# Strassen gate/up products: GpSimd sums spread out, weight conversions three products ahead, a fourth low-part buffer

## The chip, the core and the metric

The kernel runs on one core of one Trainium2 chip. The metric is the device time of one execution in microseconds (us); the median of three runs counts. The engines are written as in the profile: PE (TensorE matmul) with PEld (its weight loads), DVE (VectorE), ACT (ScalarE), POOL (GpSimd), SP (SyncE, which here issues DMAs).

## What is computed

One layer of a hybrid decoder on 512 prompt positions and 8 x 4 sample positions (544 columns in all): attention and a state-space branch, an output projection, then a SwiGLU feed-forward part, then a norm. All in float32. The change touches the last stages:

```python
hf = rms_norm(x, p['norm_ffn'][l])
x = x + (jax.nn.silu(hf @ p['w_gate'][l]) * (hf @ p['w_up'][l])) @ p['w_down'][l]
```

with a model width of 2048 and an inner width of 5632.

## The kernel before

**Precision.** A float32 operand is split in a high part (ACT copies it to float32r, "hi") and a low part (DVE subtracts, "lo"); a product is hi x hi + hi x lo + lo x hi, so three matmuls per 128x128 weight tile. `conv(u)` makes both parts of one weight block of 128x512: `wh` on ACT (L1994) and `wl` on DVE (L1995).

**Strassen.** A 256-row block of an output is made of seven products P1 to P7 (Winograd's form), each over weight blocks or sums of them. The sums of weight blocks are `sadd`: P5's and P6's on POOL (L1972, L1974), P7's and P3's on DVE (L1976, L1978). P6's sum reads P5's, P3's reads P6's. A product is a *unit*: 12 matmuls of 272 columns. Gate and up have two k halves, h0 and h1, so 14 units each, in the order `TWO`: P1.0 P5.0 P2.0 P1.1 P5.1 P6.0 P6.1 P3.0 P7.0 P7.1 P2.1 P4.0 P3.1 P4.1. In this text they are G0 to G13 for gate and U0 to U13 for up; G and U together are a *pair* of 28 units, and there are 22 pairs. Down has one half and seven units, D0 to D6 (P1 P5 P6 P2 P7 P3 P4), in 40 such groups: 32 with four k tiles (12 matmuls a unit), then 8 with three (9 matmuls a unit).

**PSUM.** P1, P6, P7 and P4 add into one bank X, P5 and P3 into Y, P2 into V. Since they add on, P7 may write X only after P6's running sum has been read out, and P4 only after P7's. The readers are *events*: in gate/up on ACT for P1, P5, P6, P7 (L2046, L2049, L2053, L2056), on DVE for P2, P3, P4; in down on ACT for P1, P5, P6 (L2178, L2182, L2187), on DVE for P2 (L2194), P7 (L2191), P3 (L2197), P4 (L2200).

**The order of the work** is written by hand. Every engine runs its instructions in the order in which `stage` emits them and waits for semaphores alone. For each unit u that is:

```python
for f in at.pop(u, ()):      # what plan_at put here
    f()
for v in sum_at.pop(u, ()):  # weight sums of later units
    sadd(v)
mms(u)
events(u - 1)
conv(u + 2)
```

`plan_at` puts the element-wise work of a pair (scaling by the norm's factor L2081, SiLU L2084, gate times up L2095, the four sums of the finished block L2107 to L2116, and the splits `one` and `two` of the forms that down will read, L387 on ACT and L388 on DVE) at chosen units; the DMA stores of those forms (`store`) too. For pairs 19 to 21 there are two plain splits (`direct`) in place of sums and splits. `AHEAD` says how many units early a sum is emitted.

**Buffers.** `wh` and `wl` rotate over three buffers each, the sums over four (tag `raw`; P6.1 has one of its own), the loaded weight halves `rw` over three. The next load is issued by `conv` of P4, which is the last reader.

Of the kernel before, what the change touches and what calls it, by code (L numbers as in the profile page):

```python
# [8 lines left out]
F32R = mybir.dt.float32r  # L9
# [3 lines left out]
ALU = mybir.AluOpType  # L13
# [4 lines left out]
P = 128  # L18
# [13 lines left out]
NK = 2  # L32
# [99 lines left out]
def hybrid_step(  # L132
# [9 lines left out]
    def nm(p):  # L142
        uid[0] += 1
        return f"{p}{uid[0]}"
# [4 lines left out]
    stream = es.enter_context(tc.tile_pool(name="stream", bufs=3))  # L149
# [7 lines left out]
    pools = {"act": actp, "ps": ps_p, "mm": mm_p}  # L157
# [1717 lines left out]
    PT = nc.gpsimd.tensor_tensor  # L1875
# [46 lines left out]
    units = []  # L1922
    raws = []

    AHEAD = {("P5", 0): 5, ("P6", 0): 8, ("P5", 1): 5, ("P6", 1): 6}
    at = {}
    sum_at = {}

    def add(g):
        gems.append(g)  # L1930
        g.u0 = len(units)
        for i, (p, h) in enumerate(g.order):
            last = all(q != p for q, _ in g.order[i + 1:])
            if p in ("P5", "P6", "P7", "P3"):
                e = AHEAD.get((p, h), 3) if len(g.halves) == 2 else 3
                sum_at.setdefault(max(len(units) - e, -1), []).append(len(units))
            units.append((g, p, h, i, last))
        for h in range(len(g.halves)):
            raws.append((g, h))
# [3 lines left out]
    def raw_dma():  # L1943
        if nraw[0] < len(raws):
            g, h = raws[nraw[0]]
            nraw[0] += 1
            k0, n, _ = g.halves[h]
            t = pools["wraw"].tile([P, 8, 256], F32, tag="wraw", name=nm("rw"))
            for a in range(0, 2 * n, 4):
                c = min(4, 2 * n - a)  # L1950
                nc.sync.dma_start(
                    out=t[:, a:a + c, :],
                    in_=g.W[(k0 + a) * P:(k0 + a + c) * P, g.c0:g.c0 + 256].rearrange("(k p) c -> p k c", p=P),
                )
            g.raw[h] = t

    def blk(g, h, i, j):
        n = g.halves[h][1]
        return g.raw[h].rearrange("p (j e) c -> p j e c", e=2)[:, 0:n, j, i * P:(i + 1) * P]

    def v128(t, n):
        return t.rearrange("p a (b c) -> p (a b) c", c=P)[:, 0:n]
# [22 lines left out]
    def conv(u):  # L1985
        if u >= len(units):
            return
        g, p, h, _, _ = units[u]
        n = g.halves[h][1]
        src = {"P1": lambda: blk(g, h, 0, 0), "P2": lambda: blk(g, h, 0, 1), "P4": lambda: blk(g, h, 1, 1)}.get(p, lambda: g.Sp.pop((p, h)))()  # L1990
        hi = stream.tile([P, NK, 256], F32R, tag="whi", name=nm("wh"))
        lo = stream.tile([P, NK, 256], F32R, tag="wlo", name=nm("wl"))
        hv, lv = v128(hi, n), v128(lo, n)
        nc.scalar.activation(out=hv, in_=src, func=AF.Copy)  # L1994
        TT(out=lv, in0=src, in1=hv.bitcast(F32), op=ALU.subtract)  # L1995
        conv_t[u] = hv, lv
        if p == "P4":
            raw_dma()

    def mms(u):  # L2000
        g, p, h, _, last = units[u]
        hv, lv = conv_t.pop(u)
        n = g.halves[h][1]
        new = BANK[p] not in g.b
        ps = g.bank(BANK[p])
        xs = [tuple(x.bitcast(F32R) for x in form(g.halves[h][2][j], FORMS[p])) for j in range(n)]
        todo = [(hv, j, x) for j in range(n) for x in xs[j]] + [(lv, j, xs[j][0]) for j in range(n)]
        for i, (w, j, x) in enumerate(todo):
            nc.tensor.matmul(ps[:, :HALF], lhsT=w[:, j, :], rhs=x, start=new and i == 0,  # L2009
                             stop=last and i == len(todo) - 1, skip_group_check=True)  # L2010
# [7 lines left out]
    def stage(u0, u1):  # L2018
        for u in range(u0, u1):
            for f in at.pop(u, ()):  # L2020
                f()
            for v in sum_at.pop(u, ()):
                sadd(v)
            mms(u)
            events(u - 1)
            conv(u + 2)
            g, _, _, i, _ = units[u]
            if i in g.hooks:
                g.hooks[i]()
            tick()  # L2030
# [37 lines left out]
    def gate_up(f):  # L2068
        gt, ut = [None] * 2, [None] * 2
        halves = [(0, 4, xforms[0:4]), (8, 4, xforms[4:8])]  # L2070

        def plan_at(u, *fs):
            for i, f_ in enumerate(fs):
                if f_ is not None:
                    at.setdefault(u + i, []).append(f_)

        def g4(g):
            TT(out=gt[1][:, L_], in0=g.b["X"][:, :HALF], in1=rbf[:, L_], op=ALU.mult)

        def scale(t):  # L2080
            return lambda: PT(out=gt[t], in0=gt[t], in1=rbf, op=ALU.mult)  # L2081

        def silu(t):
            return lambda: nc.scalar.activation(out=gt[t], in_=gt[t], func=AF.Silu)  # L2084

        def u4(g):
            TT(out=ut[1][:, L_], in0=g.b["X"][:, :HALF], in1=gt[1][:, L_], op=ALU.mult)

        def post_gate(u0):
            plan_at(u0 + 12, lambda: PT(out=gt[1][:, R_], in0=gt[1][:, R_], in1=rbf[:, R_], op=ALU.mult))  # L2090
            plan_at(u0 + 16, scale(0), silu(1), scale(1), silu(0), scale(0))

        def post_up(u0):
            plan_at(u0 + 12, lambda: PT(out=ut[1][:, R_], in0=ut[1][:, R_], in1=gt[1][:, R_], op=ALU.mult))
            plan_at(u0 + 16, lambda: PT(out=ut[0], in0=ut[0], in1=gt[0], op=ALU.mult))  # L2095
            pr = f // 2
            if pr < NPAIR:
                o = [None] * 7
                w = {}

                def store(*xs):
                    for x in xs:
                        nc.sync.dma_start(out=fd[pr, x], in_=o[x].bitcast(F32))

                def sum0():
                    w["t"], w["v"] = slot(), slot()
                    PT(out=w["t"][:, L_], in0=ut[0][:, R_], in1=ut[0][:, L_], op=ALU.subtract)  # L2107

                def sum1():
                    PT(out=w["v"][:, L_], in0=ut[1][:, R_], in1=ut[0][:, R_], op=ALU.subtract)  # L2110

                def sum2():
                    PT(out=w["t"][:, R_], in0=ut[1][:, R_], in1=w["t"][:, L_], op=ALU.subtract)

                def sum3():
                    PT(out=w["v"][:, R_], in0=ut[1][:, L_], in1=w["t"][:, R_], op=ALU.subtract)  # L2116

                def one():
                    o[0] = slot(F32R)
                    split((o[0][:, L_], o[0][:, R_]), ut[0][:, L_])  # L2120

                def two(x, src):
                    def go():
                        o[x], o[x + 1] = slot(F32R), slot(F32R)
                        split((o[x], o[x + 1]), src())
                    return go

                plan_at(u0 + 17, sum0, sum1, sum2, sum3)
                plan_at(u0 + 18, one, two(1, lambda: ut[1]), lambda: store(0, 1, 2), two(3, lambda: w["t"]),
                        two(5, lambda: w["v"]), lambda: store(3, 4, 5, 6))  # L2130
            else:
                def direct(x):
                    def go():
                        h, l = slot(F32R), slot(F32R)
                        split((h, l), ut[x])
                        for y, t in enumerate((h, l)):
                            nc.sync.dma_start(out=hd[f - (NF - NDIR) + x, y], in_=t.bitcast(F32))
                    return go
                plan_at(u0 + 17, direct(1), direct(0))

        ev = {}
        tmp_ev(ev, gt)
        ev["P4"] = g4
        add(Gem(W_G, f * P, halves, ev))
        post_gate(gems[-1].u0)
        ev = {}
        tmp_ev(ev, ut)
        ev["P4"] = u4
        add(Gem(W_U, f * P, halves, ev))
        post_up(gems[-1].u0)  # L2150

    for f in range(0, NF, 2):
# [106 lines left out]
    for c in range(nS):  # L2259
        for q in range(8):  # L2260
            g = units[nG + (c * 8 + q) * 7][0]
# [59 lines left out]
    for m in range(0, 16, 2):  # L2321
        if m == 10:
            flush()
            es_big2.close()
            pools["wraw"] = es_raw.enter_context(tc.tile_pool(name="wraw", bufs=3))
            for _ in range(3):
                raw_dma()

        def first_units(k):
            if k == 6:  # L2330
                for u in sum_at.pop(-1):
                    sadd(u)
                for u in range(2):
                    conv(u)

        run(gemm_pair(SXP, evac_ws(m), pre_piece=first_units if m == 14 else None))
# [161 lines left out]
```

## Time and profile before

| | us |
|---|---|
| median of three runs (lowest, highest) | 2196.16 (2195.12, 2199.06) |
| the profiled execution, its time | 2197.69 |
| its span on the core | 2195.8 |
| PE, PEld, DVE busy | 2065.0, 2007.4, 1848.8 |
| ACT, POOL busy | 1088.0, 1144.6 |

Gate/up runs from 696 to 1674 us, down from 1674 to 2088 us. Matmuls overlap each other, so a PE row of 12 matmuls is longer than the 1.5 us after which the next unit starts; starts are what to compare. A DVE row also runs some 0.08 us into the next one; again the distance of starts tells what the engine spends. POOL's ends are rough.

### The profile page before, as it was taken

To read this page: it belongs to the slowest core of one execution; us is meant where nothing else is said; L and a number is where in the kernel's file an instruction comes from. 1 tells how busy PE (TensorE), PEld (TensorE's weight loads), DVE (VectorE), ACT (ScalarE), POOL (GpSimd) and SP (SyncE) were. 2 spreads that over 40 slices of the span, in tenths; PEclk is the share of its full clock that TensorE was granted. 3 is DMA by queue.
4 is the path that set the end of the run, shared out by engine and by line. 5 is a ranking of instruction groups with operands and counts; after the bars stand their busy time and mean duration, and the time that the engine had idled before them with its cause. 6 is when DMAs were issued, how large, how long until landed. Compare 5 with 4: busy or idle time off the path is not lost.

```text
span 2195.8 us, 43890 instructions
## 1 busy us (share of the span) xinstructions
PE 2065.0 (94%) x16370; PEld 2007.4 (91%) x16370; DVE 1848.8 (84%) x2825; ACT 1088.0 (50%) x2277; POOL 1144.6 (52%) x1012
## 2 busy tenths in 40 slices
PE   8598899989998999999999999999999999999996
PEld 7587899879988899999999999999998999999995
DVE  7988845668577899999999999999997888888986
ACT  6143336764344455555555555555554445545564
POOL 7825433022275566656666666666655555555600
PEclk9798999999998999999999999999999999999998
DMA  6345794213342343434343434343439988977554
GB/s 187 110 131 159 230 274 126 62 59 116 116 155 90 111 154 113 152 133 166 113 151 134 166 114 151 131 162 120 151 118 320 324 287 282 345 268 237 190 162 140
DMA packets 331647, 368.46 MB, mean 168 GB/s; under 512 B 55473, under 2 KB 260249, under 8 KB 331417
## 3 DMA queue, kind: packets, MB, share of 16 engines
q1 hardware_dynamic: 330536, 363.92, 50.5%
q8 instruction: 128, 2.10, 0.4%
q0 software_dynamic: 640, 1.48, 0.2%
q14 instruction: 87, 0.70, 0.1%
q10 hardware_dynamic: 256, 0.26, 0.0%
HBM read 277.67 MB, written 88.52 MB: 167 GB/s over the span
## 4 chain that ended last, share of the span: by engine, by line
PE 62%; DVE 16%; issue 6%; ACT 2%; POOL 2%; DMA 1%; DVEq 0%; ACTq 0%; SPq 0%; POOLq 0%
PE mm L2009 44%; PE mm L293 15%; DVE wl L1995 8%; DVE sa L1976 2%; DVE s L388 1%; DVE sa L1978 1%; ACT wh L1994 1%; PE ps L1368 1%; POOL sa L1972 1%; DVE wl L263 1%; DMA rw<-in_w_up_dram 1%; PE ps L1626 0%; PE ps L1620 0%; DMA raw<-in_w_out_dram 0%; POOL s L2281 0%
## 5 line engine op out<-in xcount | busy, mean ns | idle before, releaser
L2009 PE MATMUL mm<-s,wh 128*128 128x272 f32 x7056 | 1040.0, 289 | 16.2 <-DVE s L2191 6.3
L2009 PEld LDWEIGHTS mm<-s,wh 128*128 128x128 f32 x7056 | 946.8, 189 | 23.2 <-ACT wh L1994 8.0
L2009 PE MATMUL mm<-s,wl 128*128 128x272 f32 x3528 | 597.3, 291 | 19.0 <-DVE wl L1995 17.1
L293 PE MATMUL mm<-s,wh 128*128 128x272 f32 x2816 | 508.2, 300 | 45.4 <-DVE u L1158 17.1
L2009 PEld LDWEIGHTS mm<-s,wl 128*128 128x128 f32 x3528 | 499.7, 189 | 33.2 <-DVE wl L1995 32.9
L1995 DVE TENSOR_TENSOR wl<-sa,wh 128x512 fp32r<-128x512 f32 (+1 forms) x468 | 482.0, 1040 | 53.5 <-ACT wh L1994 50.6
L293 PEld LDWEIGHTS mm<-s,wh 128*128 128x128 f32 x2816 | 418.3, 195 | 58.4 <-issue 31.7
L1995 DVE TENSOR_TENSOR wl<-rw,wh 128x512 fp32r<-128x512 f32 (+1 forms) x384 | 399.9, 1050 | 53.4 <-ACT wh L1994 52.9
L1994 ACT ACTIVATE wh<-sa 128x512 fp32r<-128x512 f32 (+1 forms) x468 | 291.5, 623 | 288.3 <-PE mm L2009 122.6
L293 PE MATMUL mm<-s,wl 128*128 128x272 f32 x1408 | 315.8, 295 | 25.3 <-DVE wl L263 25.1
L1994 ACT ACTIVATE wh<-rw 128x512 fp32r<-128x512 f32 (+1 forms) x384 | 236.7, 622 | 162.8 <-PE mm L2009 117.3
L1972 POOL TENSOR_TENSOR sa<-rw 128x512 f32<-128x512 f32 (+1 forms) x128 | 200.9, 1570 | 190.7 <-DVE wl L1995 116.1
L293 PEld LDWEIGHTS mm<-s,wl 128*128 128x128 f32 x1408 | 234.8, 195 | 27.5 <-DVE wl L263 27.5
L261 ACT ACTIVATE wh<-raw 128x512 fp32r<-128x512 f32 x200 | 124.4, 625 | 165.4 <-PE mm L293 98.1
L263 DVE TENSOR_TENSOR wl<-raw,wh 128x512 fp32r<-128x512 f32 x152 | 114.5, 758 | 82.9 <-ACT wh L261 82.7
L388 DVE TENSOR_TENSOR s<-s,s 128x544 fp32r<-128x544 f32 (+2 forms) x154 | 118.2, 784 | 40.8 <-ACT s L387 34.3
L1974 POOL TENSOR_TENSOR sa<-sa,rw 128x512 f32<-128x512 f32 (+1 forms) x84 | 138.4, 1648 | 3.1
L342 POOL TENSOR_TENSOR wl<-raw,wh 128x512 fp32r<-128x512 f32 x48 | 64.6, 1348 | 140.9 <-ACT wh L261 134.6
L2081 POOL TENSOR_TENSOR s<-s,rbc 128x544 f32<-128x544 f32 x66 | 116.6, 1791 | 8.0 <-ACT s L2084 8.0
L2058 POOL TENSOR_TENSOR s<-s,s 128x272 f32<-128x272 f32 x44 | 35.8, 814 | 162.5 <-ACT s L2056 162.5
L342 POOL TENSOR_TENSOR s<-s,s 128x512 f32<-128x512 f32 (+3 forms) x67 | 79.9, 1205 | 51.8 <-ACT s L921 37.3
L2179 POOL TENSOR_TENSOR s<-s,s 128x272 f32<-128x272 f32 x40 | 31.0, 774 | 137.6 <-ACT s L2178 126.9
(350 smaller groups left out, 2174.3 us busy)
## 6 DMA issues: line engine op xcount, KB each, us to landing
rw<-in_w_gate_dram SPq DMA_DIRECT2D x88, 512.0 KB
rw<-in_w_up_dram SPq DMA_DIRECT2D x88, 512.0 KB
rw<-in_w_down_dram SPq DMA_DIRECT2D x72, 512.0 KB
fd<-s SPq DMA_DIRECT2D x133, 272.0 KB
s<-fd SPq DMA_DIRECT2D x133, 272.0 KB
x2d<-s SPq DMA_DIRECT2D x80, 272.0 KB
s<-x2d SPq DMA_DIRECT2D x80, 272.0 KB
raw<-in_w_in_dram SPq DMA_DIRECT2D x72, 256.0 KB
```

The lines of the kernel that those rows point to most:

```text
L261: nc.scalar.activation(out=hi[:, :nk], in_=t[:, :nk], func=AF.Copy)
L263: eng.tensor_tensor(out=lo[:, :nk], in0=t[:, :nk], in1=hi[:, :nk].bitcast(F32), op=ALU.subtract)
L293: nc.tensor.matmul(ps[mt][h][:, :HALF], lhsT=w, rhs=x[:, h * HALF:(h + 1) * HALF], start=st, stop=sp)
L342: return f(*a, **kw)
L388: nc.vector.tensor_tensor(out=lo, in0=src, in1=hi.bitcast(F32), op=ALU.subtract)
L1972: PT(out=v, in0=blk(g, h, 1, 0), in1=blk(g, h, 1, 1), op=ALU.add)
L1974: PT(out=v, in0=g.S[h], in1=blk(g, h, 0, 0), op=ALU.subtract)
L1976: TT(out=v, in0=blk(g, h, 0, 0), in1=blk(g, h, 1, 0), op=ALU.subtract)
L1994: nc.scalar.activation(out=hv, in_=src, func=AF.Copy)
L1995: TT(out=lv, in0=src, in1=hv.bitcast(F32), op=ALU.subtract)
L2009: nc.tensor.matmul(ps[:, :HALF], lhsT=w[:, j, :], rhs=x, start=new and i == 0, stop=last and i == len(todo) - 1, skip_group_check=True)
L2081: return lambda: PT(out=gt[t], in0=gt[t], in1=rbf, op=ALU.mult)
```

## The change

Five edits. (1) `conv(u + 3)` instead of `conv(u + 2)`, and three blocks are converted before the first unit. (2) A fourth low-part buffer, `wlx`, for every fourth unit; the high parts keep three. (3) Weight sums are emitted four units early instead of three, P5's and P6's in gate/up five (P6's were eight and six). (4) Scaling and SiLU of gate, the product gate times up and the four sums move one unit later, with a unit left free between two scalings. (5) The form splits and their stores are spread over units 2 to 12 of the next pair, the split of block 1 first.

```diff
-    AHEAD = {("P5", 0): 5, ("P6", 0): 8, ("P5", 1): 5, ("P6", 1): 6}
+    AHEAD = {("P5", 0): 5, ("P5", 1): 5, ("P6", 0): 5, ("P6", 1): 5}
...
-                e = AHEAD.get((p, h), 3) if len(g.halves) == 2 else 3
+                e = AHEAD.get((p, h), 4) if len(g.halves) == 2 else 4
...
-        lo = stream.tile([P, NK, 256], F32R, tag="wlo", name=nm("wl"))
+        if u % 4 == 3:
+            lo = pools["wraw"].tile([P, NK, 256], F32R, tag="wlx", name=nm("wl"), bufs=1)
+        else:
+            lo = stream.tile([P, NK, 256], F32R, tag="wlo", name=nm("wl"))
...
-            conv(u + 2)
+            conv(u + 3)
...
-            plan_at(u0 + 16, scale(0), silu(1), scale(1), silu(0), scale(0))
+            plan_at(u0 + 17, silu(1), scale(0), None, scale(1), silu(0), scale(0))
...
-            plan_at(u0 + 16, lambda: PT(out=ut[0], in0=ut[0], in1=gt[0], op=ALU.mult))
+            plan_at(u0 + 17, lambda: PT(out=ut[0], in0=ut[0], in1=gt[0], op=ALU.mult))
...
-                plan_at(u0 + 17, sum0, sum1, sum2, sum3)
-                plan_at(u0 + 18, one, two(1, lambda: ut[1]), lambda: store(0, 1, 2), two(3, lambda: w["t"]),
-                        two(5, lambda: w["v"]), lambda: store(3, 4, 5, 6))
+                plan_at(u0 + 18, sum0, sum1, sum2, sum3)
+                plan_at(u0 + 16, two(1, lambda: ut[1]), None, None, None, None, one, two(3, lambda: w["t"]),
+                        lambda: store(0, 1, 2), two(5, lambda: w["v"]), None, lambda: store(3, 4, 5, 6))
...
-                plan_at(u0 + 17, direct(1), direct(0))
+                plan_at(u0 + 17, direct(1), None, direct(0))
...
-                for u in range(2):
+                for u in range(3):
                     conv(u)
```

POOL from the end of up into the next gate (pair 7's G), before. L2058 adds up two events, L1972 is P5's sum, L1974 P6's, L2094 scales half a block, L2095 is gate times up, L2107 the first of the four sums.

```order
L2058 TENSOR_TENSOR s_12526<-s_12467,s_12410 128x272
L1974 TENSOR_TENSOR sa_12532<-sa_12510,rw_12284 128x512
L2094 TENSOR_TENSOR s_12526<-s_12526,s_12259 128x272
L1972 TENSOR_TENSOR sa_12571<-rw_12507 128x512
L1974 TENSOR_TENSOR s_12590<-sa_12571,rw_12507 128x512
L2095 TENSOR_TENSOR s_12525<-s_12525,s_12258 128x544
L2107 TENSOR_TENSOR s_12645<-s_12525 128x272
```

The same place after (the lines are three later).

```order
L2061 TENSOR_TENSOR s_12530<-s_12470,s_12415 128x272
L2097 TENSOR_TENSOR s_12530<-s_12530,s_12259 128x272
L1972 TENSOR_TENSOR sa_12573<-rw_12495 128x512
L1974 TENSOR_TENSOR sa_12592<-sa_12514,rw_12265 128x512
L1974 TENSOR_TENSOR s_12612<-sa_12573,rw_12495 128x512
L2098 TENSOR_TENSOR s_12529<-s_12529,s_12258 128x544
L2110 TENSOR_TENSOR s_12671<-s_12529 128x272
```

P6.0's sum (L1974 that writes `sa`) has moved from ahead of P5.1's to behind it.

ACT ahead of G8 (P7.0), the same pair, before: conversions of P3.0, P7.0, a form split (L387), the event of P6 (L2053), the conversion of P7.1.

```order
L1994 ACTIVATE wh_12708<-sa_12668 128x512
L1994 ACTIVATE wh_12730<-sa_12693 128x512
L387 ACTIVATE s_12734<-s_12645 128x544
L2053 ACTIVATE s_12750<-mm_12592 128x272
L1994 ACTIVATE wh_12752<-sa_12716 128x512
```

After: P7.0, P7.1, a form split of half the size, the event of P6 (now L2056), P2.1.

```order
L1997 ACTIVATE wh_12710<-sa_12674 128x512
L1997 ACTIVATE wh_12727<-sa_12695 128x512
L387 ACTIVATE s_12732<-s_12529 128x272
L2056 ACTIVATE s_12747<-mm_12594 128x272
L1997 ACTIVATE wh_12749<-rw_12495 128x512
```

The conversion of P7.1 has moved ahead of P6's event.

DVE in the middle of a group of down, before: low parts of P3 and P4 (`wl`), the event of P2 (L2194), the event of P7 (L2191), the low part of the next group's P1.

```order
L1995 TENSOR_TENSOR wl_22436<-sa_22399,wh_22435 128x512
L2194 TENSOR_TENSOR s_22225<-mm_22419,s_22225 128x272
L1995 TENSOR_TENSOR wl_22457<-rw_22020,wh_22456 128x512
L2191 TENSOR_TENSOR s_22227<-mm_22349,s_22227 128x272
L1995 TENSOR_TENSOR wl_22479<-rw_22164,wh_22478 128x512
```

After, the same group: P4's low part, P2's event (now L2197), the next P1's low part, P7's event (now L2194), P5's low part.

```order
L1998 TENSOR_TENSOR wl_22440<-rw_22007,wh_22439 128x512
L2197 TENSOR_TENSOR s_22231<-mm_22423,s_22231 128x272
L1998 TENSOR_TENSOR wl_22466<-rw_22151,wh_22465 128x512
L2194 TENSOR_TENSOR s_22233<-mm_22355,s_22233 128x272
L1998 TENSOR_TENSOR wl_22485<-sa_22450,wh_22484 128x512
```

The next group's P1 has moved ahead of P7's event, and so has each low part ahead of the event that followed it.

## Rows read from the trace of the kernel before

**Rows 1.** Busy time by stretch: PE, PEld, DVE, ACT, POOL, granted clock, DMA share, GB/s

```profile
640.00:700.00 60.00, 48.53 (x344) 47.42 (x343) 40.29 (x53) 26.92 (x47) 36.67 (x29) 0.90 0.44 145
...
751.50:1589.50 838.00, 822.33 (x6387) 804.79 (x6386) 783.96 (x874) 433.84 (x799) 534.49 (x380) 1.00 0.42 141
1700.00:2010.00 310.00, 310.00 (x2478) 310.00 (x2477) 275.20 (x385) 155.49 (x294) 174.85 (x147) 1.00 0.87 297
2018.50:2086.00 67.50, 64.49 (x504) 63.16 (x503) 62.83 (x103) 36.13 (x80) 41.39 (x38) 1.00 0.58 195
```

**Rows 2.** Timeline of PE (start, length): first matmuls of pairs 7, 8, 21 and down

```profile
1017.01 1.17 PE L2009 MATMUL mm<-s,wh 128*128 128x272 f32 x8
...
1060.90 1.17 PE L2009 MATMUL mm<-s,wh 128*128 128x272 f32 x8
...
1631.59 1.17 PE L2009 MATMUL mm<-s,wh 128*128 128x272 f32 x8
...
1673.72 1.17 PE L2009 MATMUL mm<-s,wh 128*128 128x272 f32 x8
```

**Rows 3.** Timeline of PEld in pair 7: waits at G8 and U6, with releaser

```profile
1029.38 1.05 PEld L2009 LDWEIGHTS mm<-s,wh 128*128 128x128 f32 x8 [0.37 <-ACT s L2053]
...
1049.26 0.55 PEld L2009 LDWEIGHTS mm<-s,wl 128*128 128x128 f32 x4 [0.44 <-DVE wl L1995]
```

**Rows 4.** Timeline of DVE and ACT ahead of G8 in pair 7

```profile
1027.07 0.68 DVE L1976 TENSOR_TENSOR sa<-rw 128x512 f32<-128x512 f32 x1
1027.67 0.68 DVE L1995 TENSOR_TENSOR wl<-sa,wh 128x512 fp32r<-128x512 f32 x1
...
1027.86 0.63 ACT L1994 ACTIVATE wh<-sa 128x512 fp32r<-128x512 f32 x1 [1.81 <-DVE sa L1976]
1028.40 0.64 ACT L387 ACTIVATE s<-s 128x544 fp32r<-128x544 f32 x1
1028.95 0.38 ACT L2053 ACTIVATE s<-mm 128x272 f32<-128x272 f32 x1
```

**Rows 5.** Timeline of POOL and DVE in pair 7's gate, POOL busy throughout

```profile
1016.62 1.38 POOL L1972 TENSOR_TENSOR sa<-rw 128x512 f32<-128x512 f32 x1 [1.27 <-DMA rw<-in_w_gate_dram]
...
1024.07 1.26 DVE L1978 TENSOR_TENSOR sa<-rw,sa 128x512 f32<-128x512 f32 x1
1025.25 1.26 DVE L1995 TENSOR_TENSOR wl<-s,wh 128x512 fp32r<-128x512 f32 x1
```

**Rows 6.** Timeline of DVE, POOL, ACT and PE, second half of a down group

```profile
1805.44 0.43 DVE L2194 TENSOR_TENSOR s<-mm,s 128x272 f32<-128x272 f32 x1
1805.79 1.43 DVE L1995 TENSOR_TENSOR wl<-rw,wh 128x512 fp32r<-128x512 f32 x1
1807.14 0.43 DVE L2191 TENSOR_TENSOR s<-mm,s 128x272 f32<-128x272 f32 x1
1807.49 1.43 DVE L1995 TENSOR_TENSOR wl<-rw,wh 128x512 fp32r<-128x512 f32 x1
1808.84 0.43 DVE L2197 TENSOR_TENSOR s<-mm,s 128x272 f32<-128x272 f32 x1
...
1804.92 1.75 POOL L1972 TENSOR_TENSOR sa<-rw 128x512 f32<-128x512 f32 x1
1806.74 1.62 POOL L1974 TENSOR_TENSOR sa<-sa,rw 128x512 f32<-128x512 f32 x1
...
1806.23 0.63 ACT L1994 ACTIVATE wh<-rw 128x512 fp32r<-128x512 f32 x1 [0.83 <-PE mm L2009]
...
1808.03 1.16 PE L2009 MATMUL mm<-s,wh 128*128 128x272 f32 x8
```

**Rows 7.** Timeline of DVE and PE at D6 of a group with three k tiles

```profile
2035.33 0.43 DVE L2191 TENSOR_TENSOR s<-mm,s 128x272 f32<-128x272 f32 x1
...
2035.90 1.00 PE L2009 MATMUL mm<-s,wh 128*128 128x272 f32 x6 [0.44 <-DVE s L2191]
```

**Rows 8.** Timeline of PE: the wait in the first pair's unit G2

```profile
704.33 0.77 PE L2009 MATMUL mm<-s,wl 128*128 128x272 f32 x4 [1.49 <-DVE wl L1995]
```

## Prediction

> **What bounds the kernel now.** The first view is the table of busy time by stretch [rows 1]. In gate/up (751 to 1589) PE is busy 822 of 838 us and DVE 784; in down (1700 to 2010) PE is busy throughout. PE sets the pace everywhere, and DVE is close behind it in gate/up. How much can be gained is read from starts of pairs [rows 2]: pair 21, without sums and splits, takes 1673.72 - 1631.59 = 42.13 us, that is 28 units of 1.505 us with no wait; pair 7 takes 1060.90 - 1017.01 = 43.89. So a normal pair loses 1.76 us, and 19 such pairs (0 to 18) lose 33 us. That is the most that this change can win: down's groups of four k tiles have no wait to remove. The third view is PE's waits inside pair 7 [rows 3]: at G8 PE waits for P6's event on ACT (due 1017.01 + 8 x 1.505 = 1029.05, started 1029.38), at U6 for a low part on DVE.
>
> The fourth view says why DVE is late. A DVE operation with both inputs in SBUF takes 0.60 us when POOL rests (the next starts 0.60 later [rows 4]). While POOL runs it waits until POOL's instruction is done. In down the low part issued at 1807.49 leaves the engine at 1808.84; 0.60 of that is its work, so it began at 1808.24. POOL's L1974 could begin at 1807.14, when the low part before left [rows 6]. So a POOL instruction on 128x512 keeps DVE out for 1.10 us; the low part at 1805.79 gives the same (L1972 from 1805.44 to 1807.14 - 0.60 = 1806.54, again 1.10). Two DVE operations with one 128x272 POOL sum between them start 1.18 apart [rows 5], so that one claims 0.58; for 128x544 I take 1.10 x 544/512 = 1.17, an estimate. Where both queues are full the two take turns. Reading PSUM is not touched: events last 0.43 with POOL busy (0.35 to the next start) [rows 6].
>
> **The change part by part.** *What three ahead does.* The high parts still rotate over three buffers, so the high part of unit v cannot start before the hi matmuls of v - 3 are done: in down the next P1's high part starts at 1806.23, released by PE [rows 6], and neither that moment nor the fourth low buffer lets it start sooner. What moves is the order on ACT and DVE: events(u - 1) now stands behind conv(u + 2), which used to follow it. An event that PE waits for has one more conversion ahead of it, and so a wait more: for that conversion's own release, its weight sum, and POOL's turn.
>
> *Down, four k tiles.* P4 (D6) waits for P7's event. Before, the event starts at 1807.14 and ends at 1807.57, 0.46 ahead of D6 at 1808.03 [rows 6]. After, the next P1's low part stands ahead of it. If only these two change places, L1974 holds DVE out until 1808.24, the low part leaves at 1808.84, the event ends at 1809.27, and 0.14 later (the distance of event end 2035.76 and PE start 2035.90 [rows 7]) D6 starts: 1809.41 instead of 1808.03, 1.38 late. But P4's low part no longer stands behind P2's event and can be asked for 0.35 sooner (1805.79 - 1805.44 [rows 6]), and POOL's turn with it; that leaves 1.03. From below: if POOL's two sums fell wholly elsewhere, the low part would leave at 1806.23 + 0.63 + 0.60 = 1807.46, the event would end near 1807.9, and D6 would be on time. I take 1.0, near the upper row, since P5's and P6's sums keep their place in POOL's queue: 32 groups x 1.0 = **+32 us** (0 to +44). Down's other edits (sums four ahead) change no order between a sum and the conversion that reads it and cost nothing; PE's units of 1.5 us cover them.
>
> *Down, three k tiles.* PE already waits there for that event: the wait shown is 0.44 us [rows 7], and DVE is busy 62.8 of 67.5 us [rows 1]. One low part and POOL's turn more (three quarters of 0.60 + 1.10) is 1.28; with longer groups the queues ahead drain sooner, by up to 0.7. 8 x 0.75 = **+6 us** (0 to +10).
>
> *Gate: G8.* P7.0 waits for P6's event, which on ACT now stands behind P7.1's high part, and this needs P7.1's sum from DVE; before it stood behind P7.0's. I count the claims on the port from when P5.1's sum takes it, about 1016.8 [rows 5], as POOL and DVE are both full. Before, up to P7.0's sum: POOL 2 x 1.10 + 1.17 + 4 x 0.58 = 5.7; DVE five low parts and two sums 7 x 0.60, splits 0.63 and 0.35, 5.2. Sum 10.9, so 1027.7; the row shows that sum leave at 1027.67 [rows 4]. After, up to P7.1's sum: POOL has P6.0's sum more (it moved behind P5.1's, out of a stretch in which DVE had slack), 6.8; DVE has six low parts, three sums and one split of 0.63, 6.0; sum 12.8, so 1029.6. From the sum's end to PE's start it took 1029.38 - 1027.67 = 1.71 [rows 3, 4]; the split on ACT between is half as long now (0.55 becomes 0.28), so 1.44: PE starts G8 near 1031.05, 2.0 late. Before, G8 cost 0.33 and its low part as much again. So G loses 1.3 more.
>
> *Up.* The third scaling by the norm (1.17) now waits for a SiLU that stands behind P7.1's high part, so it leaves the crowd before U8, and PE's stall at G8 lets DVE catch up, by which the second up weights load earlier. The waits at U6 and U8 (with small ones, 1.76 - 0.66 = 1.1 a pair) shrink; I leave 0.5. If that load does not come earlier, the same chain as at G8 appears at U8, up to 1.6. Pair: 2.0 + 0.5 = 2.5 against 1.76, and 0.7 x 19 = **+13 us** (-33 to +40). Pairs 19 to 21 have no sums; they stay.
>
> *Start.* A third block is converted before the first unit; its high part waits for the last projection piece to free its buffer, and PSUM reads queue behind it, at least 1 us; against that the wait of 1.49 at G2 goes [rows 8]. Counted at nothing, 3 either way. Weight loads and form stores change places on SP, the loads to the front; no row shows a loss in that.
>
> The Trainium skill (SBUF — State Buffer, "Who interferes with whom") says that a DVE instruction with two SBUF inputs and a GpSimd one that reads SBUF exclude each other for the whole instruction, whoever starts first. The claims of 1.10 fit that. It does not say who is next when both wait; were it always GpSimd, a low part would wait for L1972 and L1974 in a row, and down would lose 0.4 more a group, 13 us in all; rows 6 show turns.
>
> **Sum.** 32 + 6 + 13 = +51 us. The profiled execution took 2197.69 (span 2195.8 and 1.9 around it), 1.5 above the median; I add to the median: 2196 + 51 = **2247**.
>
> **Rivals.** *Spreading works and events stay in time (faster).* If the claims at G8 fall apart, because P5.1's sum comes earlier or POOL's turns don't all meet DVE, gate/up wins up to 33 us, and if in down the low part finds the port free, nothing is lost there: 2163 to 2190. For it: DVE alone needs 0.60 a unit of 1.505; against: POOL's claims, and the order of G8. It decides where P7's sums leave DVE 1.5 us before G8. 9%. *It cancels:* both effects small, 2196. 5%. *Only down pays:* gate/up wins 23 and down loses 38: 2211. 14%. *Only gate/up pays:* the event in down keeps its margin of 0.46, 2196 + 13 = 2209. 10%. *The clock falls too:* in 640 to 700, PE busy 81%, the granted clock was 0.90, between its levels of 1.2 and 2.4 GHz; at 96% busy (2018 to 2086) it was 1.00 [rows 1]. Down after would be busy 10.5/11.5 = 91%. A mean grant of 0.95 there is a tenth of 447 us at half rate, some 22 us: 2269. 7%. The Trainium skill (TensorE: Matmul & The Clock Gate, "A second HAM failure mode: psum-queue depth-cycling") tells of a kernel whose clock swung because PE paused often between PSUM groups; that rule would make this rival the likely one, and rows 1 at 96% speak against it so far.
>
> **How the numbers follow.** The forecast (all three terms, 2230 to 2265) has 55%. A measurement of this kernel can tell about 0.2%, 4.4 us. Slower: 55 + 14 + 10 + 7 = 86%; same 5%; faster 9%. For 8 in 10 the range takes in the forecast, the two rivals near 2210 and the lower part of the clock's: 2206 to 2275.
>
> **What would show it.** In down, P7's event behind a low part that reads `rw`, PE's first row of every D6 marked with a wait for it of about 1 us, groups 11.5 instead of 10.5 us apart, PE busy 91%. In gate, P6's event on ACT right behind P7.1's high part, and PE waiting 1.5 to 2 us at G8; U6 without a wait. Wrong would be: down's groups still 10.5 apart (POOL's turns were mis-sized), or pairs under 43 us (claims don't add up as I add them).

## The result and the profile after

The changed kernel takes 2283.88 us (median of four runs, 2282.27 to 2290.62); the kernel before, on the same chip, 2197.61 (2195.12 to 2199.23). The ratio is 1.0399, interval [1.0375, 1.0424]: 86 us slower, where +51 was forecast and 2275 was the range's upper end. The direction held, the size did not.

Busy time by stretch of the kernel after, with the columns of [rows 1]: ahead of gate, pairs 1 to 19, down with four k tiles, down with three.

```profile
640.00:700.00 60.00, 48.69 (x343) 47.18 (x343) 41.09 (x54) 28.02 (x49) 35.70 (x29) 0.91 0.43 142
748.50:1629.50 881.00, 825.48 (x6384) 805.07 (x6383) 774.77 (x874) 431.06 (x799) 544.21 (x380) 1.00 0.40 134
1742.00:2060.00 318.00, 288.67 (x2258) 283.58 (x2258) 251.07 (x349) 141.64 (x268) 168.03 (x135) 1.00 0.79 269
2102.50:2172.00 69.50, 64.02 (x498) 62.62 (x498) 63.83 (x102) 35.38 (x79) 42.40 (x38) 1.00 0.56 188
```

PE has the same work and idles more: pairs 1 to 19 fill 881 us instead of 838, and in down PE is busy 288.67 of 318 us (91%), where it was busy throughout. The granted clock is 1.00 in these stretches of both kernels, so no part of the loss in them is clock.

First matmuls of pairs 8, 9, 20 and 21 and of down, PE's timeline (start, length), after; they answer [rows 2].

```profile
1074.26 0.92 PE L2012 MATMUL mm<-s,wh 128*128 128x272 f32 x6
...
1120.22 1.17 PE L2012 MATMUL mm<-s,wh 128*128 128x272 f32 x8
...
1629.68 1.17 PE L2012 MATMUL mm<-s,wh 128*128 128x272 f32 x8
...
1676.34 0.92 PE L2012 MATMUL mm<-s,wh 128*128 128x272 f32 x6
...
1720.26 1.17 PE L2012 MATMUL mm<-s,wh 128*128 128x272 f32 x8
```

Pair 8 takes 45.96 us, pair 20 46.66, pair 21 43.92; the last two took 42.13 each. In pair 20 the granted clock is 0.96 (1629.6 to 1676.3): the two units behind its wait at G8 take 2.32 each instead of 1.505, so some 1.5 us of its 4.5 are clock. By starts like these (in the last groups of down, up to the last matmul) the 85 us of span are accounted for:

| stretch | forecast | measured |
|---|---|---|
| down, 32 groups with four k tiles (346.3 to 384.3 us) | +32 | +38.0 |
| down, 8 groups with three (68.0 to 69.9) | +6 | +1.9 |
| 19 normal pairs (mean 44.10 to 46.38) | +13 | +43.3 |
| pairs 20 and 21 | 0 | +6.3 |
| ahead of gate and first pair | 0 | -3.1 |
| after down | 0 | -1.6 |
| sum | +51 | +84.8 |

What PE waits for in gate/up is in the view of waits (us in all, times, longest), PE, 748 to 1600, after:

```profile
PE mm L2012 <- ACT s L2056: 40.0, 37, 1.2
PE mm L2012 <- DVE wl L1998: 14.0, 25, 0.6
```

L2056 is P6's event, and 37 is twice in each of the 19 pairs but the last, which the window cuts. Pair 8's two places, PEld's timeline, answering [rows 3]:

```profile
1088.67 1.04 PEld L2012 LDWEIGHTS mm<-s,wh 128*128 128x128 f32 x8 [1.40 <-ACT s L2056]
...
1111.10 1.05 PEld L2012 LDWEIGHTS mm<-s,wh 128*128 128x128 f32 x8 [1.12 <-ACT s L2056]
```

They are G8 and U8. Over pairs 1 to 19 the gaps between PE's matmul starts, beyond the usual 0.125, come to a mean of 0.72 at G6, 0.31 at G7, 1.34 at G8 and 1.14 at U8; before they were 0.61 in all of G, and 0.48 and 0.39 at U6 and U8. By the starts of units a pair loses 2.97 in gate and 1.29 in up; before it lost 0.86 and 1.11. So against the kernel before gate is 2.1 us longer and up only 0.2: one wait at U8 has taken the place of two smaller ones.

The chain at U8, timelines of POOL, DVE and ACT, pair 8, after:

```profile
1098.27 1.30 POOL L1972 TENSOR_TENSOR sa<-rw 128x512 f32<-128x512 f32 x1 [2.60 <-DMA rw<-in_w_up_dram]
1099.53 1.74 POOL L1974 TENSOR_TENSOR sa<-sa,rw 128x512 f32<-128x512 f32 x1
1101.24 1.74 POOL L1974 TENSOR_TENSOR s<-sa,rw 128x512 f32<-128x512 f32 x1
1102.94 3.58 POOL L2084 TENSOR_TENSOR s<-s,rbc 128x544 f32<-128x544 f32 x2
...
1108.79 0.68 DVE L1976 TENSOR_TENSOR sa<-rw 128x512 f32<-128x512 f32 x1
1109.40 0.68 DVE L1998 TENSOR_TENSOR wl<-sa,wh 128x512 fp32r<-128x512 f32 x1
...
1109.59 0.63 ACT L1997 ACTIVATE wh<-sa 128x512 fp32r<-128x512 f32 x1 [0.57 <-DVE sa L1976]
1110.13 0.64 ACT L2087 ACTIVATE s<-s 128x544 f32<-128x544 f32 x1
1110.67 0.38 ACT L2056 ACTIVATE s<-mm 128x272 f32<-128x272 f32 x1
```

POOL runs P5.1's sum (L1972), P6.0's (L1974 that writes `sa`), P6.1's and two scalings without a pause: 3 x 1.10 + 2 x 1.17 = 5.64 by the prediction's claims. DVE has nine operations with two SBUF inputs in that time, 9 x 0.60 = 5.4. From 1098.27 these sum to 1109.3; P7.1's sum leaves DVE at 1109.40. Behind it on ACT stand P7.1's high part, a SiLU, and only then the event PE needs.

In down, DVE, POOL and PE around D6 of one group, after, answering [rows 6]:

```profile
1946.95 1.62 DVE L1998 TENSOR_TENSOR wl<-rw,wh 128x512 fp32r<-128x512 f32 x1 [0.81 <-ACT wh L1997]
1948.49 0.43 DVE L2197 TENSOR_TENSOR s<-mm,s 128x272 f32<-128x272 f32 x1
1948.84 1.43 DVE L1998 TENSOR_TENSOR wl<-rw,wh 128x512 fp32r<-128x512 f32 x1
1950.20 0.43 DVE L2194 TENSOR_TENSOR s<-mm,s 128x272 f32<-128x272 f32 x1
...
1945.77 1.01 POOL L2191 TENSOR_TENSOR s<-s,s 128x272 f32<-128x272 f32 x1 [0.17 <-ACT s L2190]
1946.73 1.29 POOL L1972 TENSOR_TENSOR sa<-rw 128x512 f32<-128x512 f32 x1
1948.10 1.62 POOL L1974 TENSOR_TENSOR sa<-sa,rw 128x512 f32<-128x512 f32 x1
...
1948.02 1.17 PE L2012 MATMUL mm<-s,wh 128*128 128x272 f32 x8
...
1950.77 1.24 PE L2012 MATMUL mm<-s,wh 128*128 128x272 f32 x8 [1.09 <-DVE s L2194]
```

The last two rows are D5 and D6: D6 was due at 1948.02 + 1.505 = 1949.53 and starts 1.24 late, behind P7's event (L2194), which stands behind the next P1's low part, which waits for POOL's L1974.

### The profile page after: what moved, and what is told of

Its sections match the earlier page's. It is cut to its first block, busy times and chain, and to the rows that moved or that the text cites. A ratio compares the mean times of both kernels' runs of the same rounds, so it can differ in the third digit from the quotient of the medians.

```text
span 2280.7 us, 43236 instructions
## 1 busy us (share of the span) xinstructions
PE 2075.6 (91%) x16370; PEld 2007.9 (88%) x16370; DVE 1843.4 (81%) x2825; ACT 1084.7 (48%) x2277; POOL 1166.1 (51%) x1012
## 4 chain that ended last, share of the span: by engine, by line
PE 49%; DVE 26%; issue 6%; ACT 5%; DMA 3%; POOL 1%; SPq 0%; ACTq 0%; DVEq 0%; POOLq 0%
PE mm L2012 32%; PE mm L293 13%; DVE wl L1998 12%; DVE sa L1978 3%; DVE sa L1976 3%; DVE s L388 2%; ACT wh L1997 2%; DMA s<-x2d 1%; DVE wl L263 1%; DMA rw<-in_w_gate_dram 1%; DVE s L2194 1%; DVE s L2197 1%; ACT s L387 1%; ACT s L2087 1%; ACT s L2056 1%
## 5 line engine op out<-in xcount | busy, mean ns | idle before, releaser
L1998 DVE TENSOR_TENSOR wl<-sa,wh 128x512 fp32r<-128x512 f32 (+1 forms) x468 | 415.2, 893 | 128.7 <-ACT wh L1997 127.7
L1998 DVE TENSOR_TENSOR wl<-rw,wh 128x512 fp32r<-128x512 f32 (+1 forms) x384 | 387.8, 1010 | 86.5 <-ACT wh L1997 82.5
L1972 POOL TENSOR_TENSOR sa<-rw 128x512 f32<-128x512 f32 (+1 forms) x128 | 192.0, 1500 | 157.5 <-DMA rw<-in_w_up_dram 62.5
L388 DVE TENSOR_TENSOR s<-s,s 128x544 fp32r<-128x544 f32 (+2 forms) x154 | 128.5, 851 | 35.5 <-ACT s L387 29.1
L2084 POOL TENSOR_TENSOR s<-s,rbc 128x544 f32<-128x544 f32 x66 | 108.5, 1656 | 85.6 <-ACT s L2087 85.6
L1974 POOL TENSOR_TENSOR sa<-sa,rw 128x512 f32<-128x512 f32 (+1 forms) x84 | 138.5, 1649 | 3.1
L2182 POOL TENSOR_TENSOR s<-s,s 128x272 f32<-128x272 f32 x40 | 42.8, 1070 | 180.5 <-ACT s L2181 166.9
L2061 POOL TENSOR_TENSOR s<-s,s 128x272 f32<-128x272 f32 x44 | 45.4, 1032 | 154.0 <-ACT s L2059 154.0
L1978 DVE TENSOR_TENSOR sa<-rw,sa 128x512 f32<-128x512 f32 (+1 forms) x84 | 112.0, 1334 | 0.0
```

What stands on the lines that cost most here:

```text
L388: nc.vector.tensor_tensor(out=lo, in0=src, in1=hi.bitcast(F32), op=ALU.subtract)
L1972: PT(out=v, in0=blk(g, h, 1, 0), in1=blk(g, h, 1, 1), op=ALU.add)
L1974: PT(out=v, in0=g.S[h], in1=blk(g, h, 0, 0), op=ALU.subtract)
L1978: TT(out=v, in0=blk(g, h, 0, 1), in1=g.S[h], op=ALU.subtract)
```

## The experiments

"Order 3" says that the events of unit u stand just ahead of conv(u + 3) on ACT and DVE, as before; order 4, just ahead of conv(u + 4), as changed. In the changed `stage` order 4 comes of `conv(u + 3)` emitted behind `events(u - 1)`. Ratios are to the kernel before on the same chip.

**Is it the lead?** (`e1_lead2`) The changed kernel with conversions two ahead again, which also restores order 3.

```diff
-            conv(u + 3)
+            conv(u + 2)
...
-                for u in range(3):
+                for u in range(2):
```

> The changed kernel with conv(u + 2) and two blocks before the first unit, all else as changed (spread work, sums four and five ahead, fourth low buffer). Theory (order): what costs is that an event that PE waits for stands behind one more conversion. Then down's groups return from 11.84 to 10.5 us, the waits at G8 and U8 (1.34 and 1.1 us) go or fall under 0.4, pairs fall from 46.1 to 43 to 44 us, and the time is 2180 to 2205 us. Rival (spread): the crowding of the port in gate/up comes from the moved GpSimd work. Then down returns to 10.5 but pairs stay near 46 us, and the time is about 2240 us.

2219.14 us, ratio 1.0092 [1.0075, 1.0110]. Down is back at 10.5 us a group and no wait for P6's event is left; but pairs take 45.47, with waits for low parts (G4 to G6, U5, U6), so the time lies between what the two theories expected. The lead, or the order that comes with it, explains down; in gate/up pairs get only 0.9 of their 2.3 us back.

**The lead alone** (`e2_lead3_alone`): the kernel before with order 4, the fourth low buffer of the changed kernel and three blocks converted ahead of the first unit.

```diff
-        lo = stream.tile([P, NK, 256], F32R, tag="wlo", name=nm("wl"))
+        if u % 4 == 3:
+            lo = pools["wraw"].tile([P, NK, 256], F32R, tag="wlx", name=nm("wl"), bufs=1)
+        else:
+            lo = stream.tile([P, NK, 256], F32R, tag="wlo", name=nm("wl"))
...
-            conv(u + 2)
+            conv(u + 3)
...
-                for u in range(2):
+                for u in range(3):
```

> The kernel before with conv(u + 3), three blocks before the first unit and the fourth low buffer, and nothing of the spread work or the earlier sums. Theory (order): down's groups are 11.8 us and pairs 45 to 47 us with waits for P6's event at G8 and U8; 2265 to 2295 us. Rival (spread): down's groups are 11.8 us, pairs stay at 43.9 us; about 2238 us.

2440.20 us, ratio 1.1092 [1.1065, 1.1120], far above both. With sums emitted three early and conversions three ahead, a sum stands in the same step as the conversion that reads it; PE waits for P6's event 4.2 us at G8 and 2.7 at U8. In down this kernel differs from the changed one in the sums' lead alone, and groups with four k tiles take 12.82 instead of 11.83, those with three 10.65 instead of 8.87: there the earlier sums, which the prediction put at nothing, are what the lead cannot do without. In gate/up it lacks the spread as well, and no run tells the two shares apart.

Part of this time is clock. From 760 to 1700 us the granted clock is 0.95 in the mean, going back and forth between its two levels; after a long wait PE's matmuls start at the lower one (PE's timeline; elsewhere these rows take 1.17 and 0.66):

```profile
1035.92 2.18 PE L2012 MATMUL mm<-s,wh 128*128 128x272 f32 x8 [4.11 <-ACT s L2056]
1037.90 1.11 PE L2012 MATMUL mm<-s,wl 128*128 128x272 f32 x4
```

Over pairs 1 to 19 the units right behind the waits run 2.1 us a pair longer than their 1.505, 40 us in all; the smaller part of that is the restart of a tenth behind each wait (last section).

**Down apart.** (`e3_down2`) The changed kernel, three ahead in gate/up and two in down.

```diff
+    nconv = [3]
...
-            conv(u + 3)
+            while nconv[0] <= u + (3 if u < nG else 2):
+                conv(nconv[0])
+                nconv[0] += 1
```

> The changed kernel with three conversions ahead in gate/up and two in down. Both theories: down's groups 10.5 us again, gate/up as changed, pairs 46.1 us: 2284 - 41 = 2243 us. If the loss of down came from what gate/up leaves behind (loads, buffers), the groups stay above 11 us and the time stays over 2265 us.

2243.85 us, ratio 1.0203 [1.0183, 1.0223]: pairs unchanged, down 411.9 us. The 40 us of down come of the lead in down, or of the order that comes with it, and not of what gate/up leaves behind.

**Lead or order?** (`e4_events_first`) The changed kernel, still three ahead, with the events of u right behind its matmuls: lead 3, order 3.

```diff
-            events(u - 1)
+            events(u)
             conv(u + 3)
...
-    events(nU - 1)
```

> The changed kernel, still three conversions ahead, but the events of unit u are emitted right after its matmuls, so that each event stands again directly ahead of conv of the unit three later. Theory (order): as with two ahead, down 10.5 us a group, no wait over 0.7 us at G8 and U8; 2180 to 2210 us. Rival (lead): converting three ahead is itself what costs (buffers, POOL's turns); then groups stay at 11.8 us and the time above 2240 us.

2196.92 us, ratio 0.9991 [0.9981, 1.0001]. In the view of waits no L2056 is left; PE, 748 to 1600:

```profile
PE mm L2012 <- DVE wl L1998: 21.2, 45, 1.3
```

Down takes 413.6 us, pairs 44.31. The whole loss goes, while conversions stay three ahead of PE's emission: in down what counts is not how early a conversion is emitted but which events stand ahead of it. On DVE in down this kernel's order is the same as before's. In gate/up the lead is not without effect: the first experiment has order 3 too, with the same sums, and takes 22 us more (pairs of 45.47 against 44.31), in waits for low parts.

**The fourth low buffer.** (`e10_three_low`) The changed kernel without it.

```diff
-        if u % 4 == 3:
-            lo = pools["wraw"].tile([P, NK, 256], F32R, tag="wlx", name=nm("wl"), bufs=1)
-        else:
-            lo = stream.tile([P, NK, 256], F32R, tag="wlo", name=nm("wl"))
+        lo = stream.tile([P, NK, 256], F32R, tag="wlo", name=nm("wl"))
```

> The changed kernel without its fourth low-part buffer: all low parts in the ring of three. Theory: high and low part of a product are written one behind the other and read by the same unit's matmuls, so the ring of three high parts already sets when a conversion can start, and the fourth low buffer gives nothing: 2280 to 2290, ratio to the kernel before 1.035 to 1.045, the waits for P6's event at G8 and U8 unchanged (1.3 and 1.0 us). Rival: the low parts are the later ones to be read, since the last matmul group of a unit reads them, and without the fourth buffer each conversion waits longer: over 2295.

2285.52 us, ratio 1.0406 [1.0380, 1.0431], as changed. The buffer does nothing here. A fourth high buffer, with which a conversion could really start sooner, was not tried, so what the lead would do then stays open.

**Order 2** (`e13_spread_events`). The kernel before with the spread hooks and events of u ahead of conv(u + 2); and, beside it, **the spread alone** (`e9_spread_alone`, edits 4 and 5 on the kernel before).

```diff
...
-            events(u - 1)
+            events(u)
             conv(u + 2)
...
```

> The same with events(u) in the place of events(u - 1): what is left out against e5_first_p6early is the lead of three, its fourth low buffer and the plain sums' one unit. If a conversion's early start has no worth while the high parts keep three buffers, this gives the time of e5_first_p6early, 2175 to 2185, or with the events ahead of the conversion a little more wait for low parts. If the lead is what takes the waits for low parts away, it stays near the kernel before, 2190 to 2205, with those waits at G5 to G8 and U6.

> The kernel before, with the spread of the SiLU, scale, store and split hooks alone (conversions still two units ahead, the sums' lead times and the events as before). Theory A: the 1.1 us per pair by which e5_first_p6early beats the kernel before (42.97 against 43.8 us) comes from the spread, since the hooks no longer stand in a cluster ahead of G8's conversion: pairs of 42.8 to 43.1 and 2172 to 2185. Theory B: it comes from the lead of three together with the events first: pairs of 43.6 to 44.0 and 2190 to 2200. The down stage stays at 414 in both.

The spread alone: 2182.44 us, ratio 0.9937 [0.9924, 0.9951], faster than before; pairs 43.32, and the waits at U6 and U8 are gone. With order 2 besides: 2262.60, ratio 1.0303 [1.0289, 1.0317], which neither theory expected. PE, 748 to 1600, order 2:

```profile
PE mm L2009 <- DVE wl L1995: 43.6, 57, 1.3
```

Now PE waits for low parts: a conversion that stands behind the event of the unit running now can't start before that unit ends. Down takes 453.9 us too. Order 3 has a loss on either side.

**P6's sums late, alone** (`e8_p6_late`), on the kernel before (`AHEAD` 5 for all).

```diff
-    AHEAD = {("P5", 0): 5, ("P6", 0): 8, ("P5", 1): 5, ("P6", 1): 6}
+    AHEAD = {("P5", 0): 5, ("P5", 1): 5, ("P6", 0): 5, ("P6", 1): 5}
```

> The kernel before with only the table of early sums changed to five for all, so that P6.0's sum stands behind P5.1's on POOL; two conversions ahead, nothing else moved. Theory (port): one more claim of 1.10 in the crowded stretch of gate, pairs from 43.8 to 44.7 to 45.1 us: 2212 to 2222 us. Rival: the place of this sum does not matter, 2195 to 2202 us.

2237.09 us, ratio 1.0182 [1.0164, 1.0200]; pairs 46.37, +2.27 where +1.1 was expected. I had counted one claim of 1.10 in gate; up has the same: the gaps between PE's matmul starts go from 0.61 to 1.53 in gate and from 0.88 to 1.89 in up. This is also what the first experiment had left: it differs from the spread alone (2182.44) in the sums' lead times and the fourth low buffer, which does nothing, and takes 37 us longer.

**P6's sums early again**, in the kernel with lead 3 and order 3 (`e5_first_p6early`), and in the changed kernel (`e14_after_p6early`).

```diff
-    AHEAD = {("P5", 0): 5, ("P5", 1): 5, ("P6", 0): 5, ("P6", 1): 5}
+    AHEAD = {("P5", 0): 5, ("P6", 0): 8, ("P5", 1): 5, ("P6", 1): 6}
...
```

The first of the two also has the edit of `e4_events_first`.

> Events right after the matmuls (as in e4_events_first) and the sums of P6 emitted eight and six units early as in the kernel before, so that P6.0's sum stands ahead of P5.1's again. Theory (port): in e4 what is left in gate are waits at G5 to G7 (1.07 us a pair) and U6 (0.45), since P6.0's sum claims the port in the crowded stretch; with its claim of 1.10 back in the stretch with slack they go, pairs fall from 44.1 to 42.4 to 43.0 us: 2165 to 2180 us. Rival (conserved): the claims are only moved, the wait turns up at other units, pairs stay at 43.7 to 44.1: 2190 to 2200 us.

> The changed kernel with P6's sums emitted eight and six units early again, as before the change; all else as changed. In gate/up the change lost 43 us in pairs 1 to 19 (44.10 to 46.38 us). Theory A: the loss comes mainly from P6's event standing behind one more conversion, P6's late sum is the smaller part (1.1 us a pair, as between e4_events_first and e5_first_p6early): pairs of 45.2, total 2255 to 2268, the waits for P6's event at G8 and U8 still there. Theory B: the late sum is the cause in gate/up (e8_p6_late, the kernel before with the late sums alone, has pairs of 46.4 too): pairs of 43.3 to 44, total 2220 to 2240, no wait for P6's event. Down stays at 454 in both.

With order 3: 2179.44 us, ratio 0.9920 [0.9907, 0.9934], faster than both kernels and not to be told from the spread alone; pairs 43.21. With order 4: 2238.60, ratio 1.0170 [1.0148, 1.0192], pairs 44.20, down 456.8. Theory B holds in its time and, within 0.2, in its pairs; its "no wait for P6's event" does not. PE, 748 to 1600, the changed kernel with P6 early:

```profile
PE mm L2012 <- ACT s L2056: 19.4, 21, 1.2
```

21 instead of 37: G8 keeps its wait (1.12 a pair), U8 has lost its own (0.11). POOL in pair 8's up there:

```profile
1084.41 1.30 POOL L1972 TENSOR_TENSOR sa<-rw 128x512 f32<-128x512 f32 x1 [1.58 <-DMA rw<-in_w_up_dram]
1085.79 1.62 POOL L1974 TENSOR_TENSOR s<-sa,rw 128x512 f32<-128x512 f32 x1
1087.37 3.58 POOL L2084 TENSOR_TENSOR s<-s,rbc 128x544 f32<-128x544 f32 x2
```

One sum fewer stands in the crowd. DVE there, P7.1's sum and the low part behind it:

```profile
1093.23 0.68 DVE L1976 TENSOR_TENSOR sa<-rw 128x512 f32<-128x512 f32 x1
1093.83 0.68 DVE L1998 TENSOR_TENSOR wl<-sa,wh 128x512 fp32r<-128x512 f32 x1
```

P7.1's sum leaves DVE at 1093.83, 10.41 after U0's start (1083.42); in the changed kernel it left 11.42 after (1109.40 - 1097.98). That is the one claim.

**Two pieces of the mechanism.** Two jobs of ACT moved behind P6's event, the second SiLU at U8 and the half-block split at G8 (`e6_silu_one_later`):

```diff
-            plan_at(u0 + 17, silu(1), scale(0), None, scale(1), silu(0), scale(0))
+            plan_at(u0 + 17, silu(1), scale(0), None, scale(1), None, silu(0), scale(0))
...
-                plan_at(u0 + 16, two(1, lambda: ut[1]), None, None, None, None, one, two(3, lambda: w["t"]),
+                plan_at(u0 + 16, two(1, lambda: ut[1]), None, None, None, None, None, lambda: (one(), two(3, lambda: w["t"])()),
```

> The changed kernel with two ACT jobs moved behind P6's event: the second SiLU one unit later (it stood ahead of the event at U8) and the form split of block 0 one unit later (it stood ahead at G8). Theory (order on ACT): the waits shrink by what stood in front, U8 from 1.1 to about 0.55 us, G8 from 1.34 to about 1.0; 22 pairs by 0.85: 2262 to 2270 us. Rival (port): PE waits for DVE's sums whatever stands between; the waits stay, 2280 to 2290 us.

2265.46 us, ratio 1.0320 [1.0299, 1.0341]; PE's wait for P6's event falls to

```profile
PE mm L2012 <- ACT s L2056: 24.1, 37, 0.9
```

The gap at U8 goes from 1.14 to 0.58, that at G8 from 1.34 to 1.03, and a new one of 0.40 at G11 takes some of it back. What stands on ACT between P7.1's high part and P6's event is on the path. And down without POOL's sums (`e7_down_no_pool_sums`), which leaves out the sums of P5 and P6 there, so that these two products read a plain weight block:

```diff
+        if len(g.halves) == 1 and p in ("P5", "P6"):
+            g.Sp[p, h] = g.S[h] = blk(g, h, 1, 0) if p == "P5" else blk(g, h, 0, 0)
+            return
```

> The changed kernel without the sums of P5 and P6 in down (part of the work is left out: these two products of down read a plain weight block). Theory (order and port together): the low part ahead of P7's event no longer waits for a turn of 1.10; groups fall from 11.84 to 10.5 to 10.7 us, those with three k tiles from 8.86 to about 7.9: 2235 to 2245 us. Rival (order alone): the conversion ahead of the event costs by its own length and release; groups stay over 11.2 us, 2260 us or more.

2243.95 us, ratio 1.0214 [1.0197, 1.0231]; groups of 10.6 us instead of 11.8 (with three k tiles 8.35 instead of 8.87, where 7.9 was expected). Order 4 alone costs down 0.1 a group; it takes POOL's claim in front of the low part to make 1.3.

## Why the prediction was right or wrong

**The sum by edits.** Two of the kernels lie between before and after. The changed kernel with order 3 and P6's sums early takes 2179.44 (-17), not to be told from the spread alone (-13). Order 4 makes 2238.60 of it (+59 by the medians; the two profiled executions, the first of them the fastest of its five, lie 68 apart: 44 in down, 20 in gate/up, 3 ahead of gate). P6's sums late make 2283.88 (+45, in gate/up, where the pair goes from 44.20 to 46.38). How the loss is shared hangs on which step is taken first: with order 3 the late sums cost 17 (2179.44 to 2196.92), and order 4 then costs 87. So the spreading pays some 13 to 17 us, as a rival said it might, and the two other edits together cost 104.

**Down, four k tiles: right, a little small.** Mechanism, place and releaser were as forecast, and the prediction's own test rows came out (groups 11.83 instead of 10.52 apart; 11.5 was named; PE busy 91%). It forecast 1.03 for D6; the row gives 1.24. The step that was short: P4's low part was asked for sooner, as said, but left 0.2 later than reckoned, since L1972 had begun only at 1946.73, behind a small POOL sum that waits for P6's event. That and 0.1 us of restart (below) make 1.32 x 28 groups, 37 us; the first two groups, which wait for other things, lost 0.2 between them, and two near the end 0.4 and 0.6.

**Down, three k tiles: too big.** +0.24 a group over the eight (8.50 to 8.74), not 0.75: of the bound of 1.28 all but 0.24 went, where I had allowed for up to 0.7. That the longer groups took it back is my account; no run shows it apart.

**Gate: right in its mechanism, a little small.** P7.1's sum was put 12.59 us after the pair's start; in pair 8 it leaves at 1087.20, 12.94 after. Units G6 to G8 lose 2.37, 2.0 was forecast. Part of this stands at G6 and G7 as waits for low parts, which I had not placed. The order on ACT is that of the forecast (DVE and ACT, pair 8, after; compare [rows 4]):

```profile
1086.59 0.68 DVE L1976 TENSOR_TENSOR sa<-rw 128x512 f32<-128x512 f32 x1
1087.20 2.35 DVE L1998 TENSOR_TENSOR wl<-sa,wh 128x512 fp32r<-128x512 f32 x2
...
1087.39 0.63 ACT L1997 ACTIVATE wh<-sa 128x512 fp32r<-128x512 f32 x1 [0.57 <-DVE sa L1976]
1087.92 0.41 ACT L387 ACTIVATE s<-s 128x272 fp32r<-128x272 f32 x1
1088.24 0.38 ACT L2056 ACTIVATE s<-mm 128x272 f32<-128x272 f32 x1
```

**Up: wrong, the step that failed.** I let U8's and the small waits shrink from 1.1 to 0.5 a pair, on the reason that the third scaling leaves the crowd and the up weights load earlier. The scaling did leave (it stands alone behind the SiLU), but I did not count what came in its place: P6.0's sum moves behind P5.1's in up exactly as in gate, a claim of 1.10, which I had entered for gate alone. Emitting P6's sums early again removes 1.03 of U8's 1.14. The weights did not come early enough to make up for it either: P5.1's sum waits 2.60 for them. What the sentence on U8 named as the other case ("the same chain as at G8 appears") is what happened. Up and the small waits were forecast 0.5 and are 4.25 - 2.37 = 1.9 a pair (4.25 is 46.38 - 42.13): 1.4 x 19 = 26 of the 34 us that are missing. Of the 1.9, up itself holds 1.29; the other 0.6 stand in gate in steps of about 0.1, half of them the restart behind a wait (below), for which I had no term. G8's 0.37 makes 7 us more. On the other side, pair 7 was a little shorter than the mean pair before (43.89 and 44.10), which takes back 4; and the pairs that carry the extra work are 1 to 19, not 0 to 18, since it runs in the pair that follows.

**Pairs 19 to 21: wrong.** "They have no sums; they stay" looked at the sums of finished blocks. The chain at G8 and U8 is made of weight sums and conversions, which every pair has; pair 20 waits 1.81 and pair 21 0.96 for the same event. That is 6 us more, of which some 1.5 are the clock in pair 20.

**Start:** -3.1 at a forecast of 0 +- 3. The first matmul of gate stands between 693 and 702 us in the traces of this case, so this is not told from noise. The wait of 1.49 at G2 did go, but one of 1.31 for P5's event (L2049) came in its place.

**The rivals.** That spreading works and the events stay in time is half true: the spread does pay by itself, but the events are late in both stages, and so neither of the rivals in which only one stage pays came in. The clock's rival fell: with PE at 91% in down and a wait of about 1.1 us for a PSUM reader in nearly every group, the granted clock is 1.00. The rule of the Trainium skill (TensorE: Matmul & The Clock Gate, "A second HAM failure mode: psum-queue depth-cycling") that I had weighed for it does not show in this kernel. A clock that swings between its levels shows in `e2_lead3_alone`, where PE waits up to 4.1 us for such a reader and the granted clock is 0.95 from 760 to 1700 us.

**The range** was too narrow because the pair's term was counted at one place, G8, and the other place with the same instructions, U8, got a smaller price without a count of its own.

## What to carry to other kernels

On in-order queues "earlier" is an order, not a time: write down which instruction now stands behind which, and count from that; here a conversion emitted a step earlier, while its buffer was free no sooner, pushed back the accumulator's readers behind it. When an edit moves one operation in a loop body that occurs twice, price it at both places. And an edit of many parts may hold a good one: here the spread alone is 0.6% faster, inside a change that is 4% slower.

## What the runs showed of the hardware

The claim of a POOL instruction on DVE held as a unit of account: counts of 1.10 (128x512), 1.17 (128x544, the estimate) and 0.60 per DVE operation gave U8's chain within 0.1 us of the row, counted afterwards, and G8's, forecast, within 0.35; one POOL sum more or fewer moved U8's chain by 1.0. When both engines are full they take turns; in the rows of down above it is L1972, low part, L1974, low part. The Trainium skill (SBUF — State Buffer, "Who interferes with whom") tells of the exclusion, with which this agrees, and not of the turns.

A wait costs PE more than the wait: the unit after it takes about 0.1 us longer. In pair 8 G8 runs from 1088.67 to the next start at 1090.28, 1.61 instead of 1.505 (the tenth stands between its first two matmuls, 0.229 apart instead of 0.125), PE's timeline:

```profile
1088.67 1.27 PE L2012 MATMUL mm<-s,wh 128*128 128x272 f32 x8 [1.17 <-ACT s L2056]
1089.78 0.66 PE L2012 MATMUL mm<-s,wl 128*128 128x272 f32 x4
1090.28 1.17 PE L2012 MATMUL mm<-s,wh 128*128 128x272 f32 x8
```

At D6 with three k tiles it is 1.22 (2121.00 to 2122.22) instead of 1.12. In gate/up the kernel before had as many waits (80 over pairs 1 to 19, and 79 after), so this hardly enters the difference; in down the wait at D6 is new, and its tenth is part of the 1.3. What PE does in that tenth no row tells.
